# Output weights split once and kept in DRAM, loaded as two parts by each output projection

## Chip, cores and metric

The kernel runs on one core of one Trainium2 chip. The metric is the device time of one launch in microseconds (us). Lower is better.

## What is computed

One hybrid decoder layer in float32 on 2048 tokens of width 1024: an input projection, two recurrent mixers on halves of its columns (HGRN2 and RWKV-7), one output projection of their concatenated results, and a convolutional feed-forward part.

```python
h = rmsnorm(x, norm1_w)
proj = h @ w_in                                   # 1024 -> 3840 columns
o_hg = hgrn2_mixer(...)                           # 512 wide
o_rw = rwkv7_mixer(...)                           # 512 wide
x = x + concat([o_hg, o_rw], -1) @ w_out          # the weights of this change: 1024 x 1024
x = x + conv_ffn(rmsnorm(x, norm2_w), ...)        # up 1024 -> 5632, conv, SiLU gate, down 2816 -> 1024
return rmsnorm(x, final_norm_w)
```

## The kernel before

**Precision.** A large matrix product is done as three matmuls on split operands. Each operand is split into a high part, which is its cast to fp32r on ScalarE (ACT), and a low part, which is the operand minus the high part, on VectorE (DVE). `mm3` (lines 270 to 272) adds high x high, high x low and low x high into one PSUM bank. `split` (lines 254 and 255) makes both parts in two new tiles; `split_to` (lines 247 and 248) writes them into tiles that exist.

**Two phases.** The first, up to about 1313 us, goes through four token blocks of 512. The second does the last block's output projection and the feed-forward part.

**The first phase.** Three streams of instructions are written out together. `dense()` holds the large products as a list of jobs. `rw_stream()` and `hg_stream()` run the recurrences of the two mixers, whose small matmuls also run on TensorE (PE). A loop at the end of `phase1` takes one step of each recurrence and then some 2000 ns of `dense()` in turn; the order of instructions on each engine is then made at build time from this order, from the data that they need and from the buffers that come free.

The jobs of one block are 30 `"P"` jobs, each with one column group of the input projection (128 columns, 24 matmuls of 512 tokens). Between them stand jobs `"T"` and `"N"` (transposes), `"E"` (a function called at this place), `"W"` (the same after a condition) and `"O"`. `"O"` is `out_block`, the output projection of an earlier block: O(0) stands ahead of block 2, O(1) ahead of block 3, and O(2) at the end. The list `extra` puts jobs in at places counted from `at[nb]`, the place where block `nb` begins.

**`out_block`** makes four passes over `k` = 0 to 7: for two halves of the block's tokens (`i2`) and two halves of the output columns (`dh`). That is 32 iterations, each with a 128 x 512 tile of `w_out` and six matmuls (two token groups `q`, three products each). In each iteration the tile is loaded (`woraw`, tag `wraw`, 4 buffers) by a DMA issued from GpSimd's queue (POOL; `wload`) and split into `wh` and `wl` (tags `wh` and `wl`, 4 buffers each). The first pass also loads the mixers' results (`oraw` from the DRAM tensor `oT`) and splits them into `hh` and `hl`. During the last pass `next_block` begins to write the next block's activations into `hh` and `hl`, which the next block's column jobs read. So each `w_out` tile is loaded and split six times over the three projections, 96 loads and splits in all, for 16 different tiles. The last block's projection, in the second phase, has code of its own and is not touched.

**The input weights** are treated otherwise. In block 0 each is loaded raw, split, and its two parts are written to DRAM tensors `Win`. Blocks 1 to 3 load the two parts straight into `wh` and `wl`, the same tags as the output projection's (`load`, line 575), one column ahead of use.

Of the kernel before, what the change touches and what calls it, by code (L numbers as in the profile page):

```python
# [7 lines left out]
F32 = mybir.dt.float32  # L8
F32R = mybir.dt.float32r
# [9 lines left out]
P = 128  # L19
T = 2048  # L20
D = 1024
KD = D // P
BLK = 512
# [44 lines left out]
def tile_layer(ctx, tc, consts, x, norm1_w, w_in, hg_lb_logits, hg_norm_w, rw_shift_mu, rw_w0, rw_w2,  # L68
# [5 lines left out]
    dma, store = nc.sync.dma_start, nc.gpsimd.dma_start  # L74

    cp = ctx.enter_context(tc.tile_pool(name="cp", bufs=1, reuse_waits="tile"))
    dp = ctx.enter_context(tc.tile_pool(name="dp", bufs=1, space=DRAM))
# [50 lines left out]
    def rstd(pool, xt, name, sqt="nsq", sqb=1):  # L128

        sq = pool.tile([P, D], BF16, tag=sqt, name="nsq", bufs=sqb)  # L130
        st = pool.tile([P, 2], F32, tag="nst", name=name, bufs=8)
        act(sq, xt, AF.Square, accum_out=st[:, 0:1])
        act(st[:, 1:2], st[:, 0:1], AF.Ln, bias=eps6, scale=1.0 / D)
        act(st[:, 1:2], st[:, 1:2], AF.Exp, scale=-0.5)
        return st[:, 1:2]
# [4 lines left out]
    with tc.tile_pool(name="vp", bufs=1, reuse_waits="tile") as vp, tc.tile_pool(name="ps0", bufs=1, space=PSUM, reuse_waits="tile") as pools["ps"]:  # L140
        rows = vp.tile([P, P], F32, name="rows")
        V.memset(rows, 0.0)
        n = 0
# [90 lines left out]
    def tdst(h, i, k0, n=1):  # L234
        v = Ts[h][i][k0 * P:(k0 + n) * P, :]
        return v if n == 1 else v.rearrange("(k p) t -> p k t", p=P)

    def four_sums(b11, b12, b21, b22):

        V.tensor_sub(b11, b12, b11)  # L240
        V.tensor_sub(b12, b22, b12)
        V.tensor_sub(b22, b22, b11)
        V.tensor_sub(b21, b21, b22)
        return b11, b22, b12, b21

    def split_to(hi, lo, src):
        c_ = S.copy(hi, src)
        return c_, V.tensor_sub(lo, src, hi.bitcast(F32))

    def split(pool, src, shape, name, bufs):  # L250

        hi = pool.tile(shape, F32R, tag=name + "h", name=name + "h", bufs=bufs)
        lo = pool.tile(shape, F32R, tag=name + "l", name=name + "l", bufs=bufs)
        S.copy(hi, src)  # L254
        V.tensor_sub(lo, src, hi.bitcast(F32))  # L255
        return hi, lo
# [11 lines left out]
    def mm3(acc, lhs, rhs, first, last, skip=False):  # L268
        (lh, ll), (rh, rl) = lhs, rhs
        TE.matmul(acc, lh, rh, start=first, stop=False, skip_group_check=skip)  # L270
        TE.matmul(acc, lh, rl, start=False, stop=False, skip_group_check=skip)  # L271
        TE.matmul(acc, ll, rh, start=False, stop=last, skip_group_check=skip)  # L272

    def phase1(c1):
        hp = c1.enter_context(tc.tile_pool(name="hp", bufs=1, reuse_waits="tile"))
        wp = c1.enter_context(tc.tile_pool(name="wp", bufs=2, reuse_waits="tile"))
# [18 lines left out]
        hl = hp.tile([P, KD, BLK], F32R, name="hl")  # L295

        def bank(kind):
            return ps.tile([P, 512], F32, tag=kind, name=kind, bufs=2)

        wload = nc.gpsimd.dma_start  # L300
# [5 lines left out]
        def stg(tag, name, bufs):  # L306
            return sp.tile([P, BLK], F32, tag=tag, name=name, bufs=bufs)
# [71 lines left out]
        def out_block(nb, oh=None, ol=None, then=None):  # L379


            for i2 in range(2):
                for dh in range(2):
                    accs = [bank("pj") for _ in range(2)]
                    for k in range(KD):
                        if i2 == 0 and dh == 0 and oh is None:
                            raw = stg("sg", "oraw", 2)
                            dma(raw, oT[nb][k * P:(k + 1) * P, :])
                            split_to(hh[:, k, :], hl[:, k, :], raw)
                        if i2 == 1 and dh == 0 and oh is not None:  # L390
                            raw = stg("sg", "oraw", 2)[:, 0:256]
                            dma(raw, oT[nb][k * P:(k + 1) * P, 256:512])
                            split_to(hh[:, k, 256:512], hl[:, k, 256:512], raw)
                        raw = wp.tile([P, 512], F32, tag="wraw", name="woraw", bufs=4)
                        wload(raw, w_out[0, k * P:(k + 1) * P, dh * 512:dh * 512 + 512])
                        wh, wl = split(wp, raw, [P, 512], "w", 4)
                        if k == KD - 2:
                            inputs = dh == 0 and (i2 == 0) == (oh is None)
                            xh = [wp.tile([P, BLK], F32, tag="wraw", name="xh", bufs=4) if inputs else
                                  stg("sg", "xh", 2) for _ in range(2)]  # L400
                            for q in range(2):
                                t0 = nb * BLK + (i2 * 2 + q) * P
                                dma(xh[q], x[0, t0:t0 + P, dh * 512:dh * 512 + 512])
                        for q in range(2):
                            is_ = slice((i2 * 2 + q) * P, (i2 * 2 + q + 1) * P)
                            lhs = ((hh[:, k, is_], hl[:, k, is_]) if oh is None or i2 == 1 else
                                   (oh[k // 4][:, k % 4, is_], ol[k // 4][:, k % 4, is_]))
                            mm3(accs[q], lhs, (wh, wl), k == 0, k == KD - 1)
                            if i2 == 1 and dh == 1 and q == 1:
                                next_block(then, k)  # L410
                            yield 680
                    for q in range(2):
                        V.tensor_add(xh[q], accs[q], xh[q])
                        r0 = (i2 * 2 + q) * P
                        (nc.gpsimd.dma_start if nb == NBLK - 2 and i2 and dh else dma)(
                            x1d[nb][r0:r0 + P, dh * 512:dh * 512 + 512], xh[q])
# [3 lines left out]
        def load4(key, src, r0):  # L420
            def f():
                rows[key] = row_tile()
                for i in range(4):
                    dma(rows[key][:, i, :], src[r0 + i * P:r0 + (i + 1) * P, :])
            return f

        def norm4(key):
            def f():
                for i in range(4):
                    t_ = rows[key][:, i, :]  # L430
                    V.tensor_scalar_mul(t_, t_, rstd(wp, t_, "nst", "wraw", 4))
            return f
# [21 lines left out]
        def next_block(nb, k):  # L454

            if nb is not None and nb < NBLK:
                for k_ in ([k - 2] if 2 <= k < KD - 1 else [k - 2, k - 1, k] if k == KD - 1 else []):
                    split_h(nb, k_)

        def sum_load(m):  # L460

            def f():
                rows[("S", m)] = [t_.rearrange("p (k t) -> p k t", k=2) for t_ in four_tiles(row_tile())]
                for i, t_ in enumerate(rows[("S", m)]):
                    dma(t_, hsrc(0, i // 2, i % 2, 2 * m, 2))
            return f

        def sum_make(m):
            def f():
                for i, t_ in enumerate(four_sums(*rows.pop(("S", m)))):  # L470
                    dma(tdst(0, i, 2 * m, 2), t_)
            return f

        def o_take(m):
# [41 lines left out]
        def dense():  # L516
# [25 lines left out]
            at = [i for i, jb in enumerate(jobs) if jb[0] == "A"]  # L542
            extra = []
            for nb in range(NBLK):
                if nb + 1 < NBLK:
                    extra += [(at[nb] + 18, ("E", load4(nb + 1, x[0], (nb + 1) * BLK))),
                              (at[nb] + 22, ("E", norm4(nb + 1))), (at[nb] + 25, ("T", nb + 1))]
                if nb >= 2:
                    extra += [(at[nb] + 6, ("E", load4(("N", nb - 2), x1d[nb - 2], 0))),
                              (at[nb] + 10, ("E", norm4(("N", nb - 2)))), (at[nb] + 11, ("N", nb - 2))]  # L550
            for m in range(2):
                extra += [(at[3] + 14 + 5 * m, ("E", sum_load(m))), (at[3] + 17 + 5 * m, ("E", sum_make(m)))]
            extra += [(at[3] + 25 + m, ("W", 2, o_take(m))) for m in range(4)]
# [27 lines left out]
            for n, jb in enumerate(jobs):  # L581
# [22 lines left out]
                _, col, ev, cond, fin = jb  # L604
# [12 lines left out]
                for k in range(KD):  # L617
                    wh, wl = ws[k // 4]
# [525 lines left out]
    with ExitStack() as c2:  # L1144
# [36 lines left out]
        with tc.tile_pool(name="op", bufs=1, reuse_waits="tile") as op_:  # L1181
# [49 lines left out]
            def weights(k, dh):  # L1231
                raw = ring("w", w_out[0, k * P:(k + 1) * P, dh * 512:dh * 512 + 512])
                wh, wl = (wo_[c].pop() if wo_[c] else
                          op_.tile([P, 512], F32R, tag="wo" + c, name="wo" + c, bufs=3) for c in "hl")
                split_next(wh, wl, raw)
                return wh, wl
# [6 lines left out]
            for dh in range(2):  # L1243
                accs = [pst("wacc") for _ in range(4)]
                for n, k in enumerate((0, 1, 4, 5, 2, 3, 6, 7)):
                    w = weights(k, dh)
# [21 lines left out]
                    for q in range(12):  # L1268
                        i, t_ = (q % 4, q // 4) if first else (q // 3, q % 3)
# [355 lines left out]
```

## Time and profile before

| | |
|---|---|
| median of 3 runs | 2646.53 us (2640.78 to 2649.34) |
| the profiled execution | 2645.42 us, of which the span from first to last instruction is 2643.6 |
| mean granted TensorE clock in it | 0.994 of full speed |
| O(0), O(1), O(2): first to last matmul | 554 to 638, 889 to 971, 1224 to 1313 us |
| casts and subtractions of the output weights, 96 each | 618 ns on ACT and 685 ns on DVE (medians) |
| DMA in the whole run | 518.98 MB, mean 196 GB/s |

In the profile's rows PE is TensorE's matmuls and PEld its weight loads; SP is the queue of SyncE, which issues most other DMAs. A row gives a line of the kernel, the engine and operation, the tile written and the tiles read, and times. An arrow in brackets names what ended the idle time ahead of a row. Matmul durations overlap (a 512-column matmul is shown with 0.39 us while the next starts 0.23 us after it).

### The profile page before, as it was taken

What the parts mean: (1) busy time and instruction counts of PE and PEld (TensorE: products, weight loads), DVE (VectorE), ACT (ScalarE), POOL (GpSimd) and SP (SyncE); (2) the same over time, 40 slices, a digit from 0 to 9 for tenths busy, and PEclk for the clock granted to TensorE, in tenths of its full rate; (3) what the DMA queues carried; (4) which work ended last, traced back from release to release, by engine and by line L of the source; (5) the groups of instructions that cost most, each with busy time, mean ns of one, the idle gap of its engine ahead of it and who ended that gap; (6) DMA issues with size and microseconds to landing.
All of it is one profiled execution on the core that took longest, in us unless ns stands there. A gap on an engine that the chain in (4) does not pass through costs nothing.

```text
span 2643.6 us, 51054 instructions
## 1 busy us (share of the span) xinstructions
PE 2547.0 (96%) x19467; PEld 2046.8 (77%) x19467; DVE 1963.7 (74%) x3744; ACT 1372.7 (52%) x2258; POOL 382.1 (14%) x686
## 2 busy tenths in 40 slices
PE   7999999999999999899899999999999999999998
PEld 5877777777777767777678888887888887888887
DVE  4868677676576765777678789988988887766556
ACT  5555444555545555344466654556554544545444
POOL 6433222212222122232100000000000000000000
PEclk9999999999999999999999999999999999999999
DMA  8846463555655565845583467747763553998655
GB/s 304 239 147 195 152 168 116 143 159 205 190 173 138 174 212 179 261 151 150 181 287 124 136 221 257 240 154 232 245 203 129 171 171 128 334 321 283 200 191 187
DMA packets 380298, 518.98 MB, mean 196 GB/s; under 512 B 114463, under 2 KB 211093, under 8 KB 380053
## 3 DMA queue, kind: packets, MB, share of 16 engines
q1 hardware_dynamic: 325521, 337.38, 40.1%
q0 software_dynamic: 54464, 178.32, 20.9%
q8 instruction: 153, 2.51, 0.4%
q14 instruction: 92, 0.75, 0.1%
q10 hardware_dynamic: 68, 0.02, 0.0%
HBM read 372.99 MB, written 134.22 MB: 192 GB/s over the span
## 4 chain that ended last, share of the span: by engine, by line
PE 70%; DVE 11%; ACT 8%; DMA 7%; issue 3%; POOL 0%; SPq 0%; DVEq 0%; ACTq 0%; POOLq 0%
PE pj L270 7%; PE pj L271 7%; PE pj L272 6%; PE ua L270 5%; PE ua L272 5%; PE ua L271 5%; PE da L271 3%; PE da L272 3%; PE da L270 3%; PE ud L271 2%; PE ud L270 2%; PE ud L272 2%; PE db L272 2%; PE db L271 2%; PE db L270 2%
## 5 line engine op out<-in xcount | busy, mean ns | idle before, releaser
L270 PE MATMUL pj<-hh,wh 128*128 128x512 f32 x960 | 391.6, 408 | 6.1 <-ACT rkv L122 4.0
L271 PE MATMUL pj<-hl,wh 128*128 128x512 f32 x960 | 377.4, 393 | 0.0
L272 PE MATMUL pj<-hh,wl 128*128 128x512 f32 x960 | 377.4, 393 | 0.0
L270 PE MATMUL ua<-Bh,uwh 128*128 128x512 f32 x704 | 276.4, 393 | 3.5 <-ACT m L122 2.2
L272 PE MATMUL ua<-Bh,uwl 128*128 128x512 f32 x704 | 274.3, 390 | 0.0
L271 PE MATMUL ua<-Bl,uwh 128*128 128x512 f32 x704 | 274.1, 389 | 0.0
L270 PEld LDWEIGHTS pj<-hh,wh 128*128 128x128 f32 x960 | 180.9, 189 | 54.5 <-issue 7.0
L272 PEld LDWEIGHTS pj<-hh,wl 128*128 128x128 f32 x960 | 180.8, 188 | 39.4 <-DMA wl<-Win171l 0.3
L271 PEld LDWEIGHTS pj<-hl,wh 128*128 128x128 f32 x960 | 181.0, 189 | 35.0 <-DVE hl L488 0.5
L254 ACT CAST uwh<-uraw 128x512 fp32r<-128x512 f32 x220 | 134.3, 617 | 135.0 <-PE ua L271 55.7
L255 DVE TENSOR_TENSOR dal<-draw,dah 128x512 fp32r<-128x512 f32 x138 | 95.2, 690 | 108.3 <-ACT dah L254 105.7
L255 DVE TENSOR_TENSOR uwl<-uraw,uwh 128x512 fp32r<-128x512 f32 x220 | 147.1, 684 | 34.3 <-ACT uwh L254 34.3
L254 ACT CAST dah<-draw 128x512 fp32r<-128x512 f32 x138 | 85.8, 621 | 160.0 <-PE da L271 75.5
L270 PEld LDWEIGHTS ua<-Bh,uwh 128*128 128x128 f32 x704 | 132.2, 188 | 33.9 <-ACT m L122 5.6
L272 PEld LDWEIGHTS ua<-Bh,uwl 128*128 128x128 f32 x704 | 132.2, 188 | 28.1 <-DVE uwl L255 0.4
L271 PEld LDWEIGHTS ua<-Bl,uwh 128*128 128x128 f32 x704 | 132.3, 188 | 26.7
L270 PE MATMUL ud<-Bh,uwh 128*128 128x512 f32 x352 | 138.0, 392 | 0.0
L1495 POOL DMA_DIRECT2D gd<-y x2 | 1.1, 542 | 943.1 <-DVE y L1493 943.1
L272 PE MATMUL ud<-Bh,uwl 128*128 128x512 f32 x352 | 137.1, 390 | 0.0
L271 PE MATMUL ud<-Bl,uwh 128*128 128x512 f32 x352 | 137.0, 389 | 0.0
L271 PE MATMUL da<-dbl,dah 128*128 128x512 f32 x332 | 129.4, 390 | 0.2 <-DVE dbl L255 0.2
L272 PE MATMUL da<-dbh,dal 128*128 128x512 f32 x332 | 129.2, 389 | 0.0
(582 smaller groups left out, 6203.0 us busy)
## 6 DMA issues: line engine op xcount, KB each, us to landing
uraw<-in_w_up_dram SPq DMA_DIRECT2D x176, 256.0 KB, 3.2
woraw<-in_w_out_dram POOLq DMA_DIRECT2D x96, 256.0 KB, 3.6
br<-gd SPq DMA_DIRECT2D x88, 256.0 KB, 4.3
draw<-Sg SPq DMA_DIRECT2D x88, 256.0 KB, 3.0
draw<-Tw SPq DMA_DIRECT2D x88, 256.0 KB, 3.9
gd<-y SPq DMA_DIRECT2D x86, 256.0 KB, 3.0
Sg<-br SPq DMA_DIRECT2D x72, 256.0 KB, 2.2
xt<-x1d SPq DMA_DIRECT2D x32, 512.0 KB, 6.5
```

The lines of the kernel that those rows point to most:

```text
L254: S.copy(hi, src)
L255: V.tensor_sub(lo, src, hi.bitcast(F32))
L270: TE.matmul(acc, lh, rh, start=first, stop=False, skip_group_check=skip)
L271: TE.matmul(acc, lh, rl, start=False, stop=False, skip_group_check=skip)
L272: TE.matmul(acc, ll, rh, start=False, stop=last, skip_group_check=skip)
L1495: (dma if end is None else nc.gpsimd.dma_start)(gd_[2 * h + b][fb * P:(fb + 1) * P, :], ys[0][:, b * BLK:(b + 1) * BLK])
```

## The change

In block 1, ahead of each of the first 16 column jobs, a new `"E"` job loads one tile of `w_out`, splits it, and writes both parts to new DRAM tensors `Wout`. `out_block` no longer loads and splits the raw tile: it loads the two parts from `Wout` straight into `wh` and `wl`. The new job takes three of the four buffers of tag `wraw` (one raw, two parts); its load is issued on POOL, its two stores on SP.

```diff
@@ out_block
-                        raw = wp.tile([P, 512], F32, tag="wraw", name="woraw", bufs=4)
-                        wload(raw, w_out[0, k * P:(k + 1) * P, dh * 512:dh * 512 + 512])
-                        wh, wl = split(wp, raw, [P, 512], "w", 4)
+                        wh, wl = (wp.tile([P, 512], F32R, tag="w" + c, name="w" + c, bufs=4) for c in "hl")
+                        for t_, src in zip((wh, wl), Wout[dh][k]):
+                            wload(t_.bitcast(F32), src)
@@ phase1, after sum_make
+        Wout = [[[dp.tile([P, BLK], F32, name=f"Wo{dh}{k}{c}") for c in "hl"] for k in range(KD)] for dh in range(2)]
+
+        def wo_split(dh, k):
+
+            def f():
+                raw = wp.tile([P, BLK], F32, tag="wraw", name="woraw", bufs=4)
+                wload(raw, w_out[0, k * P:(k + 1) * P, dh * BLK:(dh + 1) * BLK])
+                wts = [wp.tile([P, BLK], F32R, tag="wraw", name="wosp", bufs=4) for _ in range(2)]
+                split_to(*wts, raw)
+                for t_, dst in zip(wts, Wout[dh][k]):
+                    dma(dst, t_.bitcast(F32))
+            return f
@@ dense
+            extra += [(at[1] + 1 + n, ("E", wo_split(n // KD, n % KD))) for n in range(2 * KD)]
```

## The prediction, made before the changed kernel was run

> **What bounds the kernel now.** I read the page's engine rows and chain first, then busy time by stage, then the rows of the weights `woraw`, then the time order on POOL, ACT and PE around the output projection, then what PE waits for there.
>
> ```profile
> span 2643.6 us, 51054 instructions
> PE 2547.0 (96%) x19467; PEld 2046.8 (77%) x19467; DVE 1963.7 (74%) x3744; ACT 1372.7 (52%) x2258; POOL 382.1 (14%) x686
> PE 70%; DVE 11%; ACT 8%; DMA 7%; issue 3%; POOL 0%; SPq 0%; DVEq 0%; ACTq 0%; POOLq 0%
> ...
> 330.00:545.00 215.00, 208.24 (x2299) 164.56 (x2297) 149.10 (x355) 99.42 (x157) 52.00 (x96) 0.99 0.52 146
> 548.00:640.00 92.00, 84.31 (x1073) 61.68 (x1072) 72.54 (x163) 54.50 (x95) 17.21 (x32) 0.98 0.50 158
> 884.00:972.00 88.00, 81.43 (x1071) 60.34 (x1070) 71.36 (x158) 55.20 (x95) 17.15 (x32) 1.00 0.52 165
> 1213.00:1313.00 100.00, 91.88 (x1240) 71.13 (x1239) 74.28 (x186) 54.91 (x100) 16.18 (x30) 0.95 0.44 141
> ```
>
> The first three lines say that PE is busy nearly all the time and carries 70% of the chain that ended last. The last four are stages: most of token block 1, where the new splits go, and the three output projections O(0), O(1) and O(2). Their columns are the stage, its length, busy us (count) of PE, PEld, DVE, ACT and POOL, the granted clock, the DMA share and GB/s. In the projections PE stands idle for 92-84.31 = 7.7, 88-81.43 = 6.6 and 100-91.88 = 8.1 us, 22.4 us in all; nothing that only relieves ACT or DVE there can bring more.
>
> ```profile
> L395 POOL DMA_DIRECT2D woraw<-in_w_out_dram x96: 537/539/542, 285.2 to 1302.2; - x96
> L254 ACT CAST wh<-woraw x96: 602/618/626, 548.2 to 1309.6; 128x512 fp32r<-128x512 f32 x96
> L255 DVE TENSOR_TENSOR wl<-woraw,wh x96: 669/685/694, 548.8 to 1310.8; 128x512 fp32r<-128x512 f32 x96
> ...
> PE pj L270 <- ACT hh L247: 6.0, 5, 2.0
> PE pj L271 <- DVE wl L255: 2.7, 8, 1.0
> PE pj L270 <- ACT wh L254: 0.7, 2, 0.5
> ```
>
> The first rows are the work that the change takes away (ns, shortest/median/longest); the others are PE's waits over the first 1360 us (total, times, longest). PE has waited only 2.7 + 0.7 = 3.4 us for the split weights themselves, and 6.0 us for the casts of the activations, which share ACT with them.
>
> What matters more is how the weights' buffers turn over:
>
> ```profile
> 537.95 0.54 POOL L575 DMA_DIRECT2D wh<-Win280h  x1 [1.46 <-PE pj L272]
> 538.48 0.54 POOL L575 DMA_DIRECT2D wl<-Win280l  x1
> 540.67 0.54 POOL L575 DMA_DIRECT2D wh<-Win281h  x1 [1.65 <-PE pj L272]
> 541.20 0.54 POOL L575 DMA_DIRECT2D wl<-Win281l  x1
> ...
> 548.19 1.14 ACT L254 CAST wh<-woraw 128x512 fp32r<-128x512 f32 x2
> 553.95 0.48 PE L270 MATMUL pj<-wh,hh 128*128 128x512 f32 x1
> 555.11 0.71 PE L272 MATMUL pj<-wh,hl 128*128 128x512 f32 x2
> 556.71 0.61 ACT L254 CAST wh<-woraw 128x512 fp32r<-128x512 f32 x1
> 558.57 0.62 ACT L254 CAST wh<-woraw 128x512 fp32r<-128x512 f32 x1
> ...
> 637.02 0.54 POOL L575 DMA_DIRECT2D wh<-Win160h  x1 [5.89 <-PE pj L272]
> 638.12 0.40 PE L272 MATMUL pj<-wh,hl 128*128 128x512 f32 x1
> ```
>
> Columns: start, duration, engine, line, operation, and what ended the idle time before it. The first column of the next block (Win28, both halves) is loaded at 538 to 541 us, before O(0), and used only after it. So two of the four `wh`/`wl` buffers stay taken, and O(0) turns over the other two: two casts run at 548.19, the third only at 556.71, after the first iteration's last matmul (555.11 plus two starts), the fourth at 558.57. The next column (Win16) is not loaded until the projection ends. O(1) has the same order; O(2) has no column behind it and so all four buffers. Now a freed buffer is refilled from a `woraw` that lies ready in SBUF, in 0.62 + 0.69 = 1.3 us. Afterwards it is refilled from DRAM.
>
> **The change part by part.**
>
> *Splits taken away.* 96 casts x 0.618 = 59 us of ACT and 96 subtractions x 0.685 = 66 us of DVE leave the three projections; 16 of each come into block 1. On the path this is worth the 3.4 us of waits for `wh` and `wl` and, I take it, half of the 6.0 us for `hh` (the rest waits for `oraw`): -6 us. Bounds: 0 and -22.4.
>
> *Loads in their place.* Each of the 96 iterations loads two parts instead of one raw tile: 96 more issues x 0.54 = 52 us of POOL, which is busy 17 of 92 us in O(0), so the issuing itself is hidden. The landing is not. A load into `wh` now waits for the matmuls that still read that buffer, and POOL's queue stands behind it; what is queued behind are further projection loads and, after them, Win16.
>
> ```profile
> woraw<-in_w_out_dram POOLq DMA_DIRECT2D x28, 256.0 KB, 4.0
> ...
> woraw<-in_w_out_dram POOLq DMA_DIRECT2D x28, 256.0 KB, 3.7
> ...
> wh<-Win280h POOLq DMA_DIRECT2D x3, 256.0 KB, 3.1
> wl<-Win280l POOLq DMA_DIRECT2D x3, 256.0 KB, 3.2
> ...
> 888.96 0.47 PE L270 MATMUL pj<-wh,hh 128*128 128x512 f32 x1
> 967.47 0.63 PE L270 MATMUL pj<-wh,hh 128*128 128x512 f32 x2
> 967.94 0.39 PE L271 MATMUL pj<-wl,hh 128*128 128x512 f32 x1
> 968.17 0.40 PE L272 MATMUL pj<-wh,hl 128*128 128x512 f32 x1
> 970.31 0.39 PE L272 MATMUL pj<-wh,hl 128*128 128x512 f32 x1
> ```
>
> Issue to landing of 256 KB has a median of 4.0 us in O(0) and 3.7 us in O(1) (the first two rows, each from its own stage), and 3.1 and 3.2 us for a pair of column loads over the whole run. `wl` is issued 0.54 us after `wh` and needed one matmul later; matmuls start 0.23 us apart (967.94 to 968.17). So the refill takes L = 4.0 + 0.54 - 0.23 = 4.3 us in O(0) and 4.0 in O(1), or 3.4 in both at the quicker landing. I do not raise it for the extra traffic: 32 x 256 KB over 92 us adds 91 GB/s to 158.
>
> Against L stands the time from the end of an iteration to the start of the one after next. I took it from the 192 matmul rows of each projection; the first and last of O(0) (553.95 and 638.12) and of O(1) (888.96 and 970.31) are shown. Of 30 such gaps in O(0), 25 are shorter than 4.3 and 18 shorter than 3.4 (from 1.4 to 6.5 us); in O(1) 23 are shorter than 4.0 and 20 shorter than 3.4. Now two bounds. If PE keeps its order and simply stands, delaying all behind, going through the gaps one by one (each wait shifts all later rows) gives 23.7 + 21.5 = 45 us at the long refill and 13.6 + 14.3 = 28 us at the short one. If the recurrences fill every wait, an iteration only can't be shorter than half of (six matmuls, 1.38 us, plus L): 32 x 2.84 = 91 us against 84.4 in O(0), 32 x 2.69 = 86 against 81.6 in O(1), together +11 us; at the short refill 32 x 2.39 = 76 us, nothing. The four corners are 45, 28, 11 and 0. I take their mean, +21 us, since the instruction order is made anew for the changed program and will place some recurrence work in the waits, while that work comes in bursts paced by DVE. A stretched projection can't be made up for: the columns of the next block need its last pass, because that pass frees `hh`.
>
> The Trainium skill ("DMA: Bandwidth & Descriptors", section on the anatomy of one DMA) fits a GpSimd-issued transfer with about 2.0 us plus bytes over 436 GB/s. For 256 KB that is an estimate of 2.6 us and a refill of 2.9, with which PE in its present order would lose 17 us and nothing if filled, mean 9, and the sum would come to +5. This trace's medians of 3.1 to 4.0 us lie above the fit, so the rows stay; what a quick landing would do is a rival below.
>
> *O(2).* With four buffers the gap is from one iteration to the fourth after it, and none of the 28 is under 5.0 us: 0 us lost. POOL also issues block 3's stores of `oT` there, and the last of them comes 11 us after the last weight load (1302.2), so none stands behind a late one: 0, at worst one refill, 4 us.
>
> *Block 1.* 16 raw loads (POOL, 16 x 0.54 = 9 us in a queue busy 52 of 215), 16 casts (10 us of ACT), 16 subtractions (11 us of DVE) and 32 stores on SP enter the first 16 columns. PE is idle 215-208.24 = 6.8 us there beside 149 us of DVE, so it feels about 5% of DVE's work: 0.5 us. The stores stand in SP's queue behind DVE's subtraction, and the `KBT` and `E` transfers of the recurrence stand behind the stores. Added are 12.6 MB over 215 us, 59 GB/s on 146. The bounds are 0 and 11 us (all of the DVE work on the path); I take +2, near the idle share, with something for the queue. No later work waits for the DRAM copies: the last is written some 100 us before O(0) reads it.
>
> *Sum.* -6 + 21 + 0 + 2 = +17 us on the profiled execution's 2645.4, that is 2662. The median of the runs, 2646.5, is 1.1 us above that execution; I say 2663. About 0.3% (7.9 us) is what a measurement of this kernel can tell from no change.
>
> **The rivals.**
>
> *Nothing visible.* The recurrences fill the waits. For it: 2.6 us per iteration is already the pace (84.4/32), and at L = 3.9 the evenly spread pace is the same. Against it: the late part of each projection is dense (the last gap of O(0) is 1.4 us) and has little else to run. Time: 0 to 5 us of stretch, -6 and +2: 2641 to 2647.
>
> *Faster.* The projections are really held by DVE's and ACT's queues, in which the recurrence waits behind the splits. For it: DVE is busy 72.5 of 92 us in O(0), and a third of that, 32 x 0.685 = 22 us, goes. It decides if two refills are always under way early enough, which needs L below some 2.0 us (then only 6 and 7 of the 30 gaps are shorter) or four free buffers. Half of the 22.4 us of idle time goes: 2646 - 11 = 2635. Against: no landing median shown is below 3.1 us, and Win28 is loaded first.
>
> *Quick landing.*
>
> ```profile
> DMA to landing us min/median/max: 2.8/3.6/6.1
> ```
>
> If all loads landed like the quickest of the 96 now, L would be 3.1: 10.3 + 11.0 = 21 us in order, 0 if filled, mean 11, sum -6 + 11 + 2 = +7, 2653: no visible change. Against it: the median is 3.6, and the traffic grows. The Trainium skill's fit (above) points this way and further.
>
> *PE stands in order.* No filling at the long refill: 45 + 2 - 3 = +44, 2690.
>
> *The scratch ring backs up.* Each split holds three of four `wraw` buffers; two stay taken until SP's stores land. If SP stands behind the `KBT` group, the next raw load stands on POOL with the column loads behind it. Columns are loaded three half columns ahead (3 x 2.72 us, the issue spacing at 537.95 and 540.67), so PE waits only where a store is over 8 us late; at two such places of 10 us: +20 beside the forecast's +17, 2683.
>
> **How the numbers follow.** Forecast 0.50, nothing visible 0.17, quick landing 0.05, faster 0.13, PE in order 0.08, ring backs up 0.07. Of the forecast a little lies within 0.3%, since its corners reach down to 0: I move 0.02 there. That makes faster 0.13, same 0.24, slower 0.63. The range runs from 2641, the lower end of "nothing visible", to 2688, just short of PE in order; outside are most of "faster" and half of the worst case. The forecast's own range is 2651 to 2678.
>
> **What would show it.** Right: O(0) and O(1) longer by some 10 us each, with PE waits on the DMA of `wh` and `wl` that are absent now; O(2) not longer; POOL's waits before these loads ended by PE instead of DVE; ACT and DVE lighter by 49 and 55 us. Wrong: PE's idle time in the projections below 22 us, or a third and fourth buffer in use during O(0); or block 1 longer by over 5 us, which would put the loss there.

## The result, and the profile after

The changed kernel takes 2705.17 us (median; 2703.87 to 2710.55) against 2647.25 for the kernel before, a ratio of 1.0223 with a 95% interval of 1.0204 to 1.0242. It is slower, as forecast, but by 58 us where 16 were forecast, and outside the range of 2641 to 2688.

The page of the changed kernel, engine rows and chain:

```profile
span 2702.1 us, 51028 instructions
...
PE 2568.9 (95%) x19467; PEld 2059.5 (76%) x19467; DVE 1920.2 (71%) x3664; ACT 1329.2 (49%) x2178; POOL 440.2 (16%) x798
...
PE 55%; issue 16%; DMA 10%; DVE 9%; ACT 5%; POOL 4%; SPq 0%; POOLq 0%; DVEq 0%; ACTq 0%
```

Busy time by stretch for its three projections, from first to last matmul (stretch, length, busy us and count of PE, PEld, DVE, ACT and POOL, granted clock, DMA share, GB/s):

```profile
565.90:672.20 106.30, 85.99 (x1035) 60.97 (x1033) 49.57 (x113) 33.01 (x56) 33.03 (x62) 0.92 0.65 208
922.50:1028.60 106.10, 85.00 (x1035) 60.22 (x1033) 49.00 (x108) 33.29 (x57) 33.06 (x62) 0.94 0.66 208
1277.10:1364.80 87.70, 79.21 (x1055) 62.19 (x1054) 45.62 (x118) 32.24 (x60) 31.05 (x58) 0.96 0.72 240
```

The same three stretches of the kernel before:

```profile
554.00:638.40 84.40, 78.54 (x1034) 56.91 (x1033) 65.50 (x144) 49.30 (x87) 15.07 (x28) 0.98 0.51 162
889.00:970.50 81.50, 76.29 (x1034) 56.04 (x1033) 64.96 (x140) 49.84 (x86) 15.07 (x28) 1.00 0.53 168
1224.00:1312.80 88.80, 81.00 (x1055) 62.50 (x1053) 63.56 (x150) 47.56 (x86) 14.56 (x27) 0.94 0.47 150
```

ACT and DVE are each some 16 us lighter in every projection, and O(0) and O(1) are 22 and 25 us longer all the same. The chain shows 16% "issue", time for which the profile shows no wait, where it had 3%; this was not followed up. The difference of the two spans, 58.5 us, by place (times of first and last matmuls):

| stretch | before | after | difference |
|---|---|---|---|
| start to O(0) | 554.0 | 565.9 | +11.9 |
| O(0) | 84.4 | 106.3 | +21.9 |
| O(0) to O(1) | 250.6 | 250.3 | -0.3 |
| O(1) | 81.5 | 106.1 | +24.6 |
| O(1) to O(2) | 253.5 | 248.5 | -5.0 |
| O(2) | 88.8 | 87.7 | -1.1 |
| second phase | 1330.8 | 1337.3 | +6.5 |

The second phase is the same code; in all the profiled executions of this study it takes 1329 to 1338 us, whatever was changed, so its +6.5 is not laid to the change. The stretch between O(1) and O(2) takes 253.5 to 256.5 us in the three kernels whose O(2) still splits and 248.5 to 251.9 in the eleven others, so its -5.0 may belong to the splits taken away; no run tests this.

PE's longest waits in O(0) of the changed kernel (what waited, for what: us in total, times, longest):

```profile
PE pj L270 <- DMA wh<-Wo02h: 3.4, 2, 2.2
PE pj L270 <- DMA wh<-Wo11h: 2.7, 1, 2.7
PE pj L270 <- DMA wh<-Wo07h: 2.5, 2, 2.3
PE pj L270 <- DMA wh<-Wo12h: 1.7, 1, 1.7
```

A piece of the last pass of O(0) in order of time, first POOL, then PE (start, duration, engine, line, operation, and in brackets the idle time before it and what ended it):

```profile
645.88 0.54 POOL L396 DMA_DIRECT2D wl<-Wo11l  x1 [2.07 <-PE pj L272]
646.41 0.54 POOL L396 DMA_DIRECT2D wh<-Wo11h  x1
...
654.37 0.54 POOL L396 DMA_DIRECT2D wl<-Wo13l  x1 [4.63 <-PE pj L271]
```

```profile
648.45 0.40 PE L1098 MATMUL hg<-part,ones 128*128 128x512 f32 x1
651.57 0.80 PE L270 MATMUL pj<-wh,hh 128*128 128x512 f32 x1 [2.72 <-DMA wh<-Wo11h]
652.16 0.63 PE L271 MATMUL pj<-wl,hh 128*128 128x512 f32 x1
652.59 0.63 PE L272 MATMUL pj<-wh,hl 128*128 128x512 f32 x1
653.01 0.63 PE L270 MATMUL pj<-wh,hh 128*128 128x512 f32 x1
```

POOL waits for PE to free a pair, then PE for that pair to land: `wh` is issued at 646.41 and first used at 651.57. The matmul at 648.45 is the last recurrence matmul before the end of O(0); after it PE runs only the projection. And after the wait the matmuls start 0.43 us apart (652.16, 652.59, 653.01) instead of 0.23. The granted clock was 0.50 there. Busy time by stretch for the three places in O(0) where it was, and for the only one in O(0) of the kernel before:

```profile
572.40:575.70 3.30, 3.30 (x23) 2.14 (x22) 3.26 (x6) 0.97 (x2) 1.06 (x2) 0.50 0.46 148
589.50:592.80 3.30, 3.30 (x33) 1.87 (x34) 1.16 (x3) 0.00 (x0) 0.00 (x0) 0.50 0.30 103
650.90:661.10 10.20, 7.79 (x17) 5.58 (x18) 2.39 (x4) 2.22 (x3) 2.13 (x4) 0.50 0.65 239
```

```profile
566.70:570.00 3.30, 3.30 (x70) 2.36 (x69) 3.17 (x6) 2.73 (x6) 0.00 (x0) 0.50 0.35 94
```

### The profile page after: what moved, and what is told of

Read it like the earlier page. It is cut to its first block, busy times and chain, and to the rows that moved or that the text cites. A ratio compares the mean times of both kernels' runs of the same rounds, so it can differ in the third digit from the quotient of the medians.

```text
span 2702.1 us, 51028 instructions
## 1 busy us (share of the span) xinstructions
PE 2568.9 (95%) x19467; PEld 2059.5 (76%) x19467; DVE 1920.2 (71%) x3664; ACT 1329.2 (49%) x2178; POOL 440.2 (16%) x798
## 4 chain that ended last, share of the span: by engine, by line
PE 55%; issue 16%; DMA 10%; DVE 9%; ACT 5%; POOL 4%; SPq 0%; POOLq 0%; DVEq 0%; ACTq 0%
PE ua L270 5%; PE pj L270 5%; PE ua L272 4%; PE ua L271 4%; PE pj L271 4%; PE pj L272 4%; PE da L270 3%; PE da L271 3%; PE da L272 3%; PE ud L271 2%; PE ud L270 2%; PE ud L272 2%; PE db L272 2%; PE db L270 2%; PE db L271 2%
## 5 line engine op out<-in xcount | busy, mean ns | idle before, releaser
L272 PEld LDWEIGHTS pj<-hh,wl 128*128 128x128 f32 x960 | 181.3, 189 | 39.1 <-issue 0.2
```

## Experiments

All kernels below were compared with the kernel before on the same chip. Begin and length of the projections are read from their first and last matmul rows, in one profiled execution of each kernel; the end is put 0.23 us after the last matmul's start.

| kernel | begin of O(0) | O(0), O(1), O(2) us | median us | ratio to before (95%) |
|---|---|---|---|---|
| before | 554.0 | 84.4, 81.5, 88.8 | 2647 to 2650 | 1 |
| changed | 565.9 | 106.3, 106.1, 87.7 | 2705.2 | 1.0223 (1.0204 to 1.0242) |
| `a_split_only` | 571.5 | 84.8, 82.9, 90.1 | 2667.8 | 1.0072 (1.0048 to 1.0097) |
| `b_loads_only` | 555.3 | 112.2, 105.6, 90.5 | 2700.2 | 1.0194 (1.0175 to 1.0214) |
| `c_late_next` | 574.9 | 84.6, 81.6, 87.1 | 2663.6 | 1.0064 (1.0041 to 1.0087) |
| `h_three` | 568.4 | 89.3, 87.5, 88.5 | 2669.1 | 1.0064 (1.0042 to 1.0086) |
| `d_early_raw` | 558.4 | 105.3, 111.0, 90.1 | 2698.2 | 1.0200 (1.0169 to 1.0232) |
| `e_late_early` | 561.7 | 83.7, 82.8, 89.8 | 2654.5 | 1.0017 (1.0004 to 1.0030) |
| `f_first_use` | 554.4 | 89.9, 83.9, 88.9 | 2651.9 | 1.0014 (0.9999 to 1.0029) |
| `i_before_late` | 552.3 | 81.8, 83.6, 91.2 | 2654.6 | 1.0024 (1.0008 to 1.0039) |
| `g_no_loads` | 555.4 | 77.0, 77.5, 79.8 | 2628.6 | 0.9914 (0.9892 to 0.9937) |
| `m_raw_loads` | 555.2 | 77.0, 77.0, 80.6 | 2637.1 | 0.9951 (0.9936 to 0.9966) |
| `j_six_pairs` | 559.6 | 80.4, 79.3, 86.1 | 2644.7 | 0.9981 (0.9964 to 0.9998) |
| `k_first_six` | 552.5 | 86.9, 79.2, 85.9 | 2642.5 | 0.9983 (0.9967 to 0.9999) |

### Each half of the change alone

`a_split_only`: the new job in block 1 stays, `out_block` is that of before.

```diff
-                        wh, wl = (wp.tile(..., tag="w" + c, bufs=4) for c in "hl")
-                        for t_, src in zip((wh, wl), Wout[dh][k]):
-                            wload(t_.bitcast(F32), src)
+                        raw = wp.tile([P, 512], F32, tag="wraw", name="woraw", bufs=4)
+                        wload(raw, w_out[0, k * P:(k + 1) * P, dh * 512:dh * 512 + 512])
+                        wh, wl = split(wp, raw, [P, 512], "w", 4)
```

> The 16 splits and their stores stay in block 1, but the output projections load the raw tile and split it themselves as before (the stored parts are not read). If the loss adds up from two places, this keeps block 1's part alone: O(0) begins some 12 us late (near 566 instead of 554 us), O(0) and O(1) last 84 and 81 us as before, the total is 2657 to 2662 us. If instead the late start of O(0) is caused by the projections' own loads (which are issued from the same queue), O(0) begins at 554 and the total is that of before.

`b_loads_only`: no job in block 1, the projections load two parts.

```diff
-            extra += [(at[1] + 1 + n, ("E", wo_split(n // KD, n % KD))) for n in range(2 * KD)]
...
-                        for t_, src in zip((wh, wl), Wout[dh][k]):
-                            wload(t_.bitcast(F32), src)
+                        for t_, src in zip((wh, wl), stage["Win"][k][dh]):
+                            wload(t_.bitcast(F32), src.rearrange("p k c -> p (k c)"))
```

> No splits in block 1; the output projections load two ready parts for each iteration, the same bytes through the same two buffers. The parts are those of input weights that lie split in DRAM, so the projection is computed with other weights. If the two-buffer refill is the cause, O(0) and O(1) last about 106 us each (84 and 81 before), O(2) about 88, O(0) begins at 553 to 555, and the total is 2690 to 2697 us. If the loads were slow because the parts had been written not long before, or because of block 1's shifted recurrences, the projections would be near 84 us and the total near 2650.

Both came out as the adding-up theory had it, and the two excesses, 0.7% and 1.9%, add to 2.7%, a little more than the change's 2.2%. The first was larger than expected (O(0) begins at 571.5, not near 566, and the median is 6 us above the expected range), and `b_loads_only`'s median was 3 us above its range. So there are two losses in two places, and neither needs the other.

### The projections: how many pairs of buffers turn over

`c_late_next` loads the next block's first column after the projection, which leaves four pairs; `h_three` loads half of it ahead, which leaves three.

```diff
-                load(i + 1)
+                if next((j[0] for j in jobs[n + 1:] if j[0] != "E"), None) != "O":
+                    load(i + 1)
```

> The changed kernel, but the first column of the next block is loaded after the output projection instead of ahead of it, so that O(0) and O(1) have four pairs of weight buffers instead of two. Bytes and number of loads are the same. Two-buffer theory: O(0) and O(1) fall from 106 to 80 to 88 us, PE's waits on the DMA of these weights fall from some 20 us a projection to under 3, and the total is 2655 to 2665 us (block 1's loss stays, and the first column after each projection waits some 3 us). Rival, DMA bandwidth or POOL's queue: the rate of bytes is what limits, so the projections stay above 100 us and the total above 2695.

```diff
-                load(i + 1)
+                to_o = next((j[0] for j in jobs[n + 1:] if j[0] != "E"), None) == "O"
+                load(i + 1, (0,) if to_o else (0, 1))      # load() takes the halves k2 to load now
```

> The changed kernel, but only half of the next block's first column is loaded ahead of O(0) and O(1), which leaves three pairs of buffers in place of two (the changed kernel) or four. Refill theory: with three pairs an iteration's weights are refilled while two others run, so nearly the whole stretch goes: O(0) and O(1) last 84 to 90 us, PE's waits on these loads are 2 to 8 us over both, total 2660 to 2672 us (block 1's loss stays). Rival, a rate limit that fell with four pairs for another reason (order of POOL's queue): the projections lie half way, 92 to 98 us, total 2680 to 2690.

Busy time by stretch for O(0), of `c_late_next` and then of `h_three`:

```profile
574.90:659.50 84.60, 78.63 (x1035) 58.04 (x1033) 49.21 (x113) 32.13 (x57) 33.06 (x62) 0.96 0.77 250
```

```profile
568.40:657.70 89.30, 79.94 (x1035) 56.55 (x1033) 49.04 (x113) 32.21 (x57) 33.15 (x62) 0.98 0.77 247
```

PE's longest waits in O(0) of `c_late_next`:

```profile
PE pj L270 <- DMA wh<-Wo17h: 1.5, 1, 1.5
PE rw L849 <- ACT ZT L122: 1.5, 1, 1.5
PE pj L270 <- ACT hh L247: 1.2, 1, 1.2
```

With the same number of loads, O(0) goes 106, 89, 85 us for two, three and four pairs, and PE's waits on the loads of the output weights over all three projections go 41, 13 and 6 us. With four pairs the DMA moves 250 GB/s instead of 208. So it was not a limit on bytes or on POOL's queue: two pairs can't cover a refill from DRAM. `c_late_next`'s median is in its expected range and `h_three`'s too, but with three pairs PE still waited 11.5 us on these loads over O(0) and O(1), where 2 to 8 were expected.

`i_before_late` is the kernel before with the same edit.

> The kernel before with one change: the next block's first column is loaded after O(0) and O(1) instead of ahead of them, so its projections have four pairs of split buffers. It shows whether the remedy that works in the changed kernel is worth anything alone. Theory (in the kernel before a freed pair is refilled in 1.3 us from a tile that lies in SBUF, so two pairs are enough): O(0) and O(1) 82 to 85 and 79 to 82 us, total 2642 to 2650. Rival (two pairs were already too few before): both 4 us shorter or more, total below 2640.

O(0) is 3 us shorter and O(1) and O(2) 2 us longer, and the total came out 4.6 us above the range expected: four pairs alone win nothing for the kernel before.

### Block 1: where the cast stands

`d_early_raw` loads each raw tile one job ahead of its split.

```diff
             def f():
-                raw = wp.tile([P, BLK], F32, tag="wraw", name="woraw", bufs=4)
-                wload(raw, w_out[...])
+                if n < 2 * KD:
+                    rows[("wo", n)] = wp.tile([P, BLK], F32, tag="wraw", name="woraw", bufs=4)
+                    wload(rows[("wo", n)], w_out[...])
+                if n > 0:
+                    raw = rows.pop(("wo", n - 1))
...
```

> The changed kernel, but in block 1 each raw tile is loaded one column ahead of its split instead of right ahead of it. Theory: block 1 lost 13 us because the cast stands first in ACT's queue waiting for its load to land (26 us in 9 waits) and the recurrence's evictions stand behind it. Then those waits fall below 8 us, O(0) begins at 554 to 560 instead of 566, and the total is 2692 to 2700 us. Rival, the work itself or its traffic (32 stores, 16 loads) is the price: O(0) still begins near 566 and the total stays near 2705.

Waits around the splits, of the changed kernel and then of `d_early_raw`:

```profile
ACT wosp L247 <- DMA woraw<-in_w_out_dram: 26.5, 9, 5.0
DVE wosp L248 <- ACT wosp L247: 14.5, 8, 4.6
```

```profile
ACT wosp L247 <- DMA woraw<-in_w_out_dram: 2.0, 1, 2.0
ACT wosp L247 <- DMA Wo03h<-wosp: 5.2, 1, 5.2
```

The waits for landings fall from 26.5 to 2.0 us and O(0) begins at 558.4. What such a wait does is seen in the order on ACT and DVE. In the changed kernel, ACT's row first:

```profile
295.70 0.62 ACT L247 CAST wosp<-woraw 128x512 fp32r<-128x512 f32 x1 [3.40 <-DMA woraw<-in_w_out_dram]
292.98 1.06 DVE L822 STREAM_TRANSPOSE TZ<-Ti 128x512 f32<-128x512 f32 x1
296.35 0.69 DVE L248 TENSOR_TENSOR wosp<-woraw,wosp 128x512 fp32r<-128x512 f32 x1 [2.30 <-ACT wosp L247]
297.07 2.90 DVE L828 STREAM_TRANSPOSE TTs<-TZ 32x512 f32<-32x512 f32 x4
```

The same two steps of the recurrence in the kernel before:

```profile
285.52 1.03 DVE L808 STREAM_TRANSPOSE TZ<-Ti 128x512 f32<-128x512 f32 x1
286.59 2.90 DVE L814 STREAM_TRANSPOSE TTs<-TZ 32x512 f32<-32x512 f32 x4
```

`TTs` followed `TZ` at 1.07 us. Now a subtraction stands between them; it waits 2.30 us for its cast, which waited 3.40 us for its tile to land, and `TTs` follows at 4.09 us. So this one landing puts the recurrence back by 3.0 us.

The four kernels that load a raw tile right ahead of its split begin O(0) at 565.9 to 574.9 us, the three that load it a job earlier at 558.4 to 561.7, and those without splits in block 1 at 552.3 to 555.4. So by the means of these groups about 10 of some 16 us are won back by loading a job earlier. That the waiting itself was the price is not shown: ACT's idle time ahead of the casts hardly fell, from 35.7 to 34.2 us, since in `d_early_raw` eight waits, 29.0 us in all, are for stores that still read the ring's buffers (the `Wo03h` row is the longest). Why these cost less, and how the remaining 6 us divide between them and the work itself, was not tried.

### Both remedies, and what the splits are worth

`e_late_early` has the edits of `c_late_next` and `d_early_raw`. `f_first_use` has that of `c_late_next`, and splits in O(0):

```diff
+                        if nb == 0 and i2 == 0:
+                            raw = ...; wload(raw, w_out[...])
+                            wh, wl = split(wp, raw, [P, 512], "w", 4)
+                            for t_, dst in zip((wh, wl), Wout[dh][k]):
+                                dma(dst, t_.bitcast(F32))
+                        else:
...                                # the loads of the changed kernel; its jobs in block 1 go
```

> Both remedies on the changed kernel: four pairs of weight buffers in O(0) and O(1) (the next column loaded after the projection), and each raw tile of block 1 loaded one column ahead of its split. If the two losses are separate and add up, O(0) begins near 558 us and O(0) and O(1) last 84 and 82 us, and the total is 2646 to 2655 us: the loss of 58 is gone, and nothing is won over the kernel before. If the splits that were taken away had been worth something, the total would be 2635 to 2643.

> The changed kernel with four pairs of buffers in the projections, and with the splits moved out of block 1 into the first half of O(0): there each raw tile is loaded and split as in the kernel before and its two parts also stored; the second half of O(0), O(1) and O(2) load the parts. 80 instead of 96 splits are saved and block 1 is that of before. Theory: O(0) begins at 554, lasts 83 to 88 us (its 16 stores wait in SP's queue beside the loads of the mixers' results), O(1) 82; total 2642 to 2650 us. Rival, any extra DMA traffic in the projections costs: O(0) above 92 us and a total above 2655.

All but some 4 us of the loss is gone in both (ratios 1.0017 and 1.0014), and nothing is won: the likelier of the forecasts for each, though `f_first_use` is 1.9 us above its range and its O(0) pays 5 us. Is there nothing to win, then? Two bounds:

```diff
# g_no_loads: the changed kernel without block 1's jobs; wh, wl loaded only where k == 0, used for all eight k
# m_raw_loads: the same in the kernel before, whose raw tile is still loaded in each iteration
```

> Neither splits nor, but for one pair per pass of eight iterations, loads of output weights: the projections use one pair of parts of input weights for all iterations of a pass, so their sums are of other weights; 88 of 96 pairs of loads and all 96 splits are left out. It bounds what the output weights' handling costs the kernel before. Theory (it is hidden there): O(0), O(1) and O(2) are 0 to 5 us shorter each than 84, 82 and 89, total 2632 to 2646 us. Rival, the splits hold up the recurrence through ACT's and DVE's queues: 8 us shorter or more each, total below 2625.

> The kernel before with its 96 raw loads kept, but nothing reads them: the 96 splits are left out, and each pass uses one loaded pair of input weights' parts for all its iterations, so the sums are of other weights. Between it and the kernel without loads and splits (O's of 77, 77 and 80 us, total 2628.6) stands the price of the loads' traffic; between it and the kernel before, that of the splits on ACT and DVE. Theory: the splits were most of it, so the O's last 77 to 80 us and the total is 2627 to 2635. Rival, the loads' traffic was: the O's stay at 82 to 88 us and the total at 2640 to 2650.

O(0) of `m_raw_loads` and of `g_no_loads`:

```profile
555.20:632.20 77.00, 74.83 (x1035) 56.26 (x1033) 48.33 (x112) 32.11 (x57) 3.19 (x6) 1.00 0.31 99
```

```profile
555.40:632.40 77.00, 74.77 (x1034) 56.22 (x1033) 48.32 (x112) 32.10 (x57) 3.21 (x6) 1.00 0.33 99
```

Without splits O(0) takes 77.0 us in both. But that says nothing about traffic: POOL issued 6 DMAs in this stretch in both kernels, and the 32 unread raw loads of each projection were issued long ahead, in clumps, since nothing but each other's landing held them back. As a test of loads inside the projections `m_raw_loads` is void. Both runs do show that splits, waits for weights and the weights' traffic together cost the kernel before 20 us over its three projections (7.4 + 4.0 + 9.0 by `g_no_loads`). `m_raw_loads`' median missed its range by 2 us. In `g_no_loads` O(0) and O(2) are shorter by more than the 0 to 5 us of the theory, near the rival's 8, and O(1) by 4.0; its median lies between the two ranges.

The last two runs ask what eats this gain when the splits are really gone: every third iteration takes its pair from the four idle buffers of the raw tiles, on top of `e_late_early` and of `f_first_use`.

```diff
-                        wh, wl = (wp.tile([P, 512], F32R, tag="w" + c, name="w" + c, bufs=4) for c in "hl")
+                        wh, wl = (wp.tile([P, 512], F32R, tag="wraw" if k % 3 == 2 else "w" + c, name="w" + c, bufs=4)
+                                  for c in "hl")
```

> The kernel with both remedies (four pairs, raw tiles loaded early) with every third iteration's pair in the four buffers of the raw tiles, which the projections no longer use: up to six pairs. If late landings are what still eats the gain of the splits taken away, PE's waits on these loads fall from 8 us to under 2 and the O's from 84, 83 and 90 to about 78 to 81 us: total 2636 to 2646. If it is the doubled traffic, slowing the other loads of the projections, nothing changes: 2650 to 2656.

> The kernel that splits at first use in O(0), with four pairs, and every third later pair in the buffers of the raw tiles, up to six pairs. Late landings theory: O(1) and O(2) fall from 84 and 89 to 78 to 81 us, O(0) by half as much, total 2632 to 2644, faster than the kernel before. Traffic theory: total 2647 to 2653, as with four pairs.

O(0) and O(1) of `j_six_pairs`:

```profile
559.60:640.00 80.40, 75.44 (x1035) 56.39 (x1033) 48.63 (x112) 32.19 (x57) 30.90 (x58) 1.00 0.80 258
893.20:972.50 79.30, 75.10 (x1034) 56.82 (x1033) 47.34 (x107) 32.97 (x57) 30.89 (x58) 1.00 0.81 264
```

PE's waits on the weights' loads in the first phase fall from 8.4 us in `e_late_early` to 1.9, and O(0) and O(1) to 80 and 79 us, at the highest DMA rates shown here; O(2), expected at 78 to 81, stays at 86 in both kernels. Late landings had eaten much of the gain. `j_six_pairs` and `k_first_six` are 5.4 and 7.6 us below the median of the kernel before, with ratios of 0.9981 (0.9964 to 0.9998) and 0.9983 (0.9967 to 0.9999): just faster, and less than the 20 us that the bound left. Part of the rest shows in PE's waits for `hh`, the casts of the mixers' results, over the first 1360 us of `g_no_loads` and then of `j_six_pairs` (6.0 us in the kernel before):

```profile
PE pj L270 <- ACT hh L247: 3.9, 6, 1.6
```

```profile
PE pj L270 <- ACT hh L247: 11.3, 10, 2.9
```

The `oraw` tiles that these casts read land in 2.7 (the kernel before), 2.6 and 3.7 us (medians). So the traffic rival is not dead: with six pairs the loads of the weights no longer make PE wait, but other loads beside them land later. No run tests this apart.

## Why the prediction was wrong

*The mechanism in the projections was right.* Two of four pairs are held by the next column; refilling the others from DRAM takes longer than most gaps; O(0) and O(1) stretch and O(2), with four pairs, does not (predicted 0, measured -1.1). `c_late_next` and `h_three` show it.

*The term of +21 for the loads was mis-sized: O(0) and O(1) grew by 46.5.* The step that failed is the choice of the mean of four corners "since the instruction order is made anew". It was made anew, but the recurrences filled little. In O(0) of the kernel before the last recurrence matmul comes after 27.2 of the 32 iterations, in the changed kernel after 25.0 (O(1): 27.2 and 24.0). The recurrences moved up by two or three iterations and then ran out. PE stood 19.7 us in O(0) and 19.4 in O(1) for the output weights' loads, 39.1 in all. The corner of PE in order, 45, was the near one; as a rival it had a chance of 0.08.

*That 46.5 is so near 45 is chance.* PE's idle time rose by only 14.4 us in O(0) and 15.9 in O(1) (length minus busy: 20.3 and 21.1 against 5.9 and 5.2), since its other waits there fell from 11.1 to 2.3 us. The other 7.5 and 8.7 us are busy time: as many matmuls, taking longer. The prediction had no term for that. The granted clock fell from 0.98 to 0.92 in O(0) and from 1.00 to 0.94 in O(1); an estimate from these and the lengths is 8.5 + 6.4 - 1.7 = 13 us of the 16.2. The Trainium skill ("TensorE: Matmul & The Clock Gate", Part 1 and the section on oscillation) states that the array falls to half clock after some 3.4 us without work, and gives 426.7 ns between 512-column matmuls then; the rows above agree with the second, 0.43 us, but show it after a wait of only 2.72 us, and the measurement decides here.

*The refill itself was sized about right, by errors that cancel.* From the end of the matmuls that free a pair to the first use of its refill, iterations for which PE waited took a median of 4.5 us in O(0) and 4.2 in O(1) (predicted 4.3 and 4.0). But the loads of `wh` landed in 3.3 and 3.2 us (medians), not 4.0 and 3.7, while `wl` was issued ahead of `wh` and not behind it (645.88 and 646.41 above), so that `wh` went out a median of 0.76 us after its buffer came free.

*Block 1: +2 predicted, +11.9 measured.* The step that failed is pricing the splits by DVE's share of PE's idle time. It looked at the work and not at the place in the queue: the raw load is issued right ahead of the cast that needs it, and what is ordered behind the cast and its subtraction runs later, as the `TTs` rows show. The prediction's own sign of being wrong, block 1 longer by over 5 us, came true. The rival of the ring that backs up was right in that POOL stood 30 us in all ahead of the raw loads, and wrong in what it held up: PE waited for no column's load in block 1, but ACT and DVE waited for the split's.

*The splits taken away: -6 taken; the changed kernel can't tell it.* PE's other waits in O(0) and O(1) fell by 8.8 us, but a longer wait for the weights hides shorter ones. The bound of 22.4 us of idle time is near what `g_no_loads` wins, 20, but partly by luck: PE's idle time in the three projections falls from 18.9 to 9.5 us there, and the other 11 us are busy time, which the bound didn't count. The gain appears only as far as the weights land in time, none with four pairs (the three projections of `e_late_early` sum to 256.3 us, those of the kernel before to 254.7), and 9 us with six (`j_six_pairs`, 245.8).

## What to carry to other kernels

Before replacing recomputation by a reload, count the buffers that really turn over, taking off those held by the next stage: buffers minus one, times the work per buffer, must cover the refill, and with something to spare. By the mean work of 2.6 us an iteration three pairs would have done (5.3 against 4.3), yet PE still waited 11.5 us: probably because the mean hides short iterations and late landings (up to 6.7 us in `h_three`'s O(0)). Where an instruction will wait, price all that is ordered behind it on its engine, and take the order as it stands unless the rows show other work that is ready. Put a load at least one stage ahead of the first instruction that reads it, even where that engine has time to spare: here it won back about 10 us of O(0)'s late begin.

## What the runs showed of the hardware

In the changed kernel the half clock came with waits of 2.2 to 2.9 us. In O(0) and O(1) it was granted in five stretches, two of 3.4, two of 6.8 and one of 10.2 us; each began within 0.7 us of the end of such a wait, and the longest lasted through a further wait of 1.75 us. A wait of 2.35 us in O(1) brought none. In O(0) 26 of the 192 output matmuls show a duration of about 0.6 us or more, 5 in the kernel before. So 14.4 us more of idle time came with 7.5 us more of busy time. `j_six_pairs`, where no wait in O(0) and O(1) was over 1.3 us, had the full clock throughout both. The waits are not the only way to it: O(2) of the kernel before, with no waits on these loads, was granted 0.94.

With six pairs all DMA together moved 264 GB/s in O(1): the rate of 208 GB/s in the changed kernel was an effect of the waits, not their cause.
